# Splitting both last-phase projection weights once, in token block 2, and keeping the halves in DRAM

## The chip, the cores and the metric

The kernel runs on one core of a Trainium2 chip, in one launch. The metric is device time in microseconds (us), the median of several runs. The engines are named as in the profile: PE (matrix engine), PEld (its weight loads), DVE (vector engine), ACT (scalar engine), POOL (GpSimd) and SP (the sync engine, which issues all DMAs of this kernel; its rows read SPq).

## The reference

A decoder block over 2048 tokens of 1024 channels, all in float32. Both branches read one normalised and modulated input through one input projection. Cut to what matters here:

```python
h = _rmsnorm(x, norm_g[l]) * (1.0 + scale[:, None, :]) + shift[:, None, :]
p = jnp.einsum('bsd,de->bse', h, w_in[l])
c_val, c_gate, c_og, ts, r_og, g_conv, g_rwkv = jnp.split(p, SPLITS, axis=-1)
y_conv = _conv_branch(c_val, c_gate, c_og, ..., w_conv_out[l])   # ends in u @ w_conv_out
y_rwkv = _rwkv7_branch(ts, r_og, ..., w_rwkv_out[l])             # ends in o @ w_rwkv_out
m = jax.nn.sigmoid(g_conv) * y_conv + jax.nn.sigmoid(g_rwkv) * y_rwkv
out = jnp.einsum('bsd,de->bse', m, w_out[l])
x = x + gate[:, None, :] * out
return _rmsnorm(x, final_g)
```

The convolution branch ends in a layer norm over channels and a gate; the RWKV branch is a recurrence over tokens with a state of 64 x 64 per head, a group norm and a gate.

## The kernel before

Tokens are worked in four blocks of 512 (b = 0 to 3). A float32 product is made of three products of halves: every weight and every activation is split into a high half (a cast to fp32r) and a low half (the difference), and `mm3` adds hi x hi, hi x lo and lo x hi. A weight of 128 output channels is a tile of 128 x 1024 values (0.5 MB).

The first phase runs over the blocks. Each makes its input h (`hprep`, from x that `xnorm` normalised and stored a block earlier), then goes through four groups (g) of four heads: `pair` projects k, r and v and prepares the chunks of the recurrence; `group` inverts small triangular matrices on POOL (through DRAM: dA, La, dT) and runs the recurrence; `fill` does convolution (`conv`) and gate (`gates`) projections beside it. Input weights are split in block 0 and kept in DRAM (`KEPT`); later blocks load both halves (kh_in, kl_in, lines 168 and 169). The buffers called hx (seven of 128 x 512) serve the normalisation of x. In block 1 they also serve `ogate`, which multiplies the output weight by its gate, splits it and stores the halves (kh_o, kl_o): in each group two weights, each in two pieces of 128 x 512, here called halves of a weight. Block 3 has no next block to normalise, and does the first parts of the last phase's block 0 there.

The last phase starts while the last recurrence ends. For each block: `osplit` (RWKV output, gate, split), `lnorm` (layer norm of the convolution, gate, split), `rproj` (product with w_rwkv_out, eight weights, "ro"), `cproj` (with w_conv_out, eight weights, "co"), and the output product ("pout", eight pieces of weight, 48 products each) with the final norm (`addx`, `finish`). `rproj` and `cproj` call `load_w`, which for "ro" and "co" loads the weight (line 172), casts the high half on ACT (line 175) and subtracts on DVE (line 177), in every block anew. High, low and unsplit tiles share six buffers (tag "w", `WB = 6`).

Inside each engine instructions run in a fixed order. It is made when the kernel is built, by a scheduler that estimates times; `tc.high_priority` moves an instruction ahead. DMAs are issued by SP in its order, and an issue that waits for its source or its buffer holds all those behind it.

Of the kernel before, what the change touches and what calls it, by code (L numbers as in the profile page):

```python
# [9 lines left out]
F32 = mybir.dt.float32  # L10
F32R = mybir.dt.float32r
I32 = mybir.dt.int32
AF = mybir.ActivationFunctionType
ALU = mybir.AluOpType
# [4 lines left out]
P = 128  # L19
D = 1024  # L20
KT = D // P
# [26 lines left out]
def lplan(t):  # L48
    n = {"c": 0, "g": 0}
    r = []  # L50
    for part in t.split():
        l = []
        for w in part:
            if w != "-":
                l.append(("1234" if w == "g" else w, n[w]))
                n[w] += 1
        r.append(l)
    return r
# [24 lines left out]
def hybrid_block(ctx: ExitStack, tc: tile.TileContext, x, vecs, convk, w2a2, final_g, ada, w_in, w_co, w_ro, w_o, crow, out,  # L83
                 seq=2048, groups=(0, 1, 2, 3), phase2=True, dbg=None):
    nc = tc.nc
# [6 lines left out]
    dp = ctx.enter_context(tc.tile_pool(name="dp", bufs=1, space=DRAM))  # L92
# [43 lines left out]
    wsrc = {"in": w_in, "co": w_co, "ro": w_ro, "o": {(cb, kh): w_o[cb, kh] for cb in range(4) for kh in range(2)}}  # L136
# [6 lines left out]
    kept = {}  # L143
# [3 lines left out]
    def ogate(n, half):  # L147

        back = kept.setdefault(("o", n), [dp.tile([P, KT, P], F32R, name=f"k{p_}_o{n[0]}_{n[1]}", tag=f"k{p_}_o{n[0]}_{n[1]}")
                                          for p_ in "hl"])  # L150
        hs = slice(half * 4, half * 4 + 4)
        st, gr, hi, lo = hx("w_st"), hx("w_gr"), hx("w_hi"), hx("w_lo")
        nc.sync.dma_start(st.rearrange("p (k n) -> p k n", k=4), wsrc["o"][n][:, hs, :])
        nc.sync.dma_start(gr[:, :256], grow_d[n[0] * 256:n[0] * 256 + 256].unsqueeze(0).broadcast_to([P, 256]))
        s4 = st.rearrange("p (k n) -> p k n", n=256)
        nc.gpsimd.tensor_tensor(out=s4, in0=s4, in1=gr[:, :256].unsqueeze(1).broadcast_to([P, 2, 256]), op=ALU.mult)
        nc.scalar.copy(hi.bitcast(F32R), st)
        nc.gpsimd.tensor_tensor(out=lo.bitcast(F32R), in0=st, in1=hi, op=ALU.subtract)
        for d_, s_ in zip(back, (hi, lo)):
            nc.sync.dma_start(d_[:, hs, :].bitcast(F32), s_.rearrange("p (k n) -> p k n", k=4))  # L160
# [151 lines left out]
    for g in range(4):  # L312
        s_ = c1.tile([P, 2, P], F32, name=f"S{g}")
# [3 lines left out]
    def hx(name):  # L317
        return xp.tile([P, TB], F32, name=name, tag="hx")

    def xnorm(b, tts=range(NTT)):  # L320
        for tt in tts:
            t0 = b * TB + tt * P
            ss = e2.tile([P, 8], F32, name="ss")
            xh = []
            for half in range(2):
                xt = hx("xt")
                nc.sync.dma_start(xt, x[t0:t0 + P, half * TB:half * TB + TB])
                nc.scalar.activation(hx("xsq"), xt, AF.Square, accum_out=ss[:, half:half + 1])
                xh.append(xt)
            vs, rs = ss[:, 2:3], ss[:, 3:4]  # L330
            nc.vector.tensor_tensor(out=vs, in0=ss[:, 0:1], in1=ss[:, 1:2], op=ALU.add)
            nc.vector.tensor_scalar(out=vs, in0=vs, scalar1=1.0 / D, scalar2=RMS_EPS, op0=ALU.mult, op1=ALU.add)
            rsqrt(rs, vs, e2, nc.vector, ss[:, 4:5])
            for kh in range(2):
                nc.vector.tensor_scalar(out=xh[kh], in0=xh[kh], scalar1=rs, scalar2=None, op0=ALU.mult)
                pt = pl.tile([P, 4, P], F32, name="late", tag="late")
                for i in range(4):
                    nc.tensor.transpose(pt[:, i, :], xh[kh][:, i * P:(i + 1) * P], ident)
                xo = hx("xTs").rearrange("p (a b) -> p a b", a=4)
                for i in range(4):  # L340
                    k = kh * 4 + i
                    nc.scalar.activation(xo[:, i, :], pt[:, i, :], AF.Identity, scale=g_col[:, k:k + 1],
                                         bias=shift_col[:, k:k + 1])
                nc.sync.dma_start(xT_dram[b][:, kh * 4:kh * 4 + 4, tt * P:(tt + 1) * P], xo)
# [10 lines left out]
    def hprep(b):  # L355
        h = ([], [])
        for k in range(KT):
            hf = hx("hf")
            nc.sync.dma_start(hf, xT_dram[b][:, k, :])
            hsplit(h, k, hf)  # L360
        return h
# [454 lines left out]
    def z_first(js):  # L816
        for j in js:
            z, bt = hx("z"), hx("zb")
            nc.sync.dma_start(z, o_dram[0][j])
            nc.sync.dma_start(bt, bv_dram[0][j])  # L820
            nc.gpsimd.tensor_tensor(out=z, in0=z, in1=bt, op=ALU.add)
            rt = hx("zr")
            nc.sync.dma_start(rt, ro_dram[0][j])
            nc.gpsimd.tensor_tensor(out=z, in0=z, in1=rt, op=ALU.mult)
            nc.sync.dma_start(z_dram[j], z)

    def lora_split(h):

        lf, ll, lx = hx("lora"), hx("lora_lo"), hx("lora_x")
        shifted(h, T_LORA, lf)  # L830
        nc.scalar.activation(lf[0:64], lf[0:64], AF.Tanh)
        lw = e1.tile([P, TB], F32R, name="lw", tag="lw")
        la = e1.tile([P, TB], F32R, name="la", tag="la")
        lo_, hi_ = slice(0, 64), slice(64, 128)
        for dst, sl, os_ in ((lw, lo_, hi_), (la, hi_, lo_)):
            nc.scalar.copy(dst[sl], lf[sl])
            nc.vector.tensor_tensor(out=ll[sl], in0=lf[sl], in1=dst[sl].bitcast(F32), op=ALU.subtract)
            nc.sync.dma_start(lx[os_], ll[sl])
            nc.scalar.copy(dst[os_], lx[os_])
        return lw, la  # L840
# [3 lines left out]
    def ada_steps():  # L844
        for k, _ in enumerate(ada_cols(srow, l3, "As", ASB, [((k, 8 + k), (mod[:, k:k + 1], mod[:, 8 + k:9 + k]))
                                                             for k in range(KT)])):
            ks, gs = slice(k, k + 1), slice(8 + k, 9 + k)
            nc.vector.tensor_tensor(out=shift_col[:, ks], in0=mod[:, ks], in1=ab[:, ks], op=ALU.add)
            nc.vector.tensor_tensor(out=g_col[:, ks], in0=mod[:, gs], in1=ab[:, gs], op=ALU.add)
            nc.vector.scalar_tensor_tensor(out=g_col[:, ks], in0=g_col[:, ks], scalar=1.0, in1=vc("norm_g", k),  # L850
                                           op0=ALU.add, op1=ALU.mult)
            yield

    for b in range(NB):
        h = hprep(b) if b else hprep0(x0, ada_steps())
        lora = lora_split(h)
        for g in groups:
            if b + 1 < NB:
                xnorm(b + 1, XN[g])
            else:  # L860
                z_first(ZN[g])
                if g < 3:
                    lnorm_first(g)
            if b + 1 < NB:
                todo = [(w, 2 * g + m) for w, m in (FIRST if b == 0 and g == 0 else NEXT)]
            else:
                todo = [wj for i in range(g, 4 if g < 3 else 5) if i == g or g == 3 for wj in lplan(LP)[i]]

            if b == 1:
                for _ in range(2):  # L870
                    n_ = later.pop(0)
                    for half in range(2):
                        ogate(n_, half)

            def fill(step, n=None):
                for _ in range(n or (FILL0[step] if b == 0 and g == 0 else 0)):
                    w, j = todo.pop(0)
                    if w == "c":
                        conv(b, h, j)
                    else:  # L880
                        gates(b, h, j, w)

            wcount[0] = WSH
            group(b, g, h, lora, fill)
            if b == 0 and g == GG:
                for _ in ada_cols(srow, l3, "As", ASB, [((16 + k, 17 + k), (hgate_col[:, k:k + 1], hgate_col[:, k + 1:k + 2]))
                                                        for k in range(0, KT, 2)]):
                    pass
                nc.vector.tensor_tensor(out=hgate_col, in0=hgate_col, in1=ab[:, 16:24], op=ALU.add)
                nc.vector.tensor_scalar(out=hgate_col, in0=hgate_col, scalar1=0.5, scalar2=None, op0=ALU.mult)  # L890
                nc.sync.dma_start(grow_d.rearrange("(n p) -> p n", p=P), hgate_col)
            wcount[0] = WDVE
            if todo:
                fill(0, len(todo))
# [75 lines left out]
    hl = ctx.enter_context(tc.tile_pool(name="hl", bufs=1, reuse_waits="tile"))  # L970
# [54 lines left out]
    for b in range(NB):  # L1025
# [7 lines left out]
        for tt in range(NTT):  # L1033
            xh = []
            for half in range(2):
                n = 2 * tt + half
# [97 lines left out]
```

## Time and profile before

| | us |
|---|---|
| time, median of 3 runs | 3144.74 (3140.74 to 3146.39) |
| span of the profiled execution, first to last instruction | 3131.2 |
| token block 1 of the first phase (672 to 1272) | 600 |
| token block 2 of the first phase (1272 to 1866) | 594 |
| last phase, from about 2494 to the end | 637 |

The profile gives the profiled execution's span; its time around the span isn't shown apart, and the median lies 13.5 us above the span. A row of the stretches gives its length, the busy time of each engine with the count of its instructions, the granted clock of PE (1.00 is full speed), the busy share of the DMA engines and what they moved. A row of waits reads: who waited, for whom, us in total, times, longest. A row in order of time reads: start, length, engine and line, operation, output and inputs, count, and the idle time before with what ended it.

### The profile page before, as it was taken

The page shows a single profiled execution, that of the slowest core. Times are in us where ns is not written, and L with a number is a line of the kernel's source. Part 1 is how long each engine was busy: PE and PEld are TensorE (multiplying, and loading weights), DVE is VectorE, ACT ScalarE, POOL GpSimd, SP SyncE. Part 2 cuts the span into 40 slices and gives each one's busy share as a digit, 9 for nine tenths or more (in the row PEclk, how much of TensorE's full clock was granted, in tenths as well). Part 3 has the DMA queues.
Part 4 walks back from the last instruction along what each step waited for, and adds up shares of the span by engine and source line. Part 5 has one row for each costly group of instructions (what it writes and reads, how often), then busy time and mean ns, then how long its engine had stood idle before and what let it go on. Part 6 is the DMA issues. An engine that isn't in the chain of part 4 may idle for free.

```text
span 3131.2 us, 64840 instructions
## 1 busy us (share of the span) xinstructions
PE 2990.4 (96%) x25672; PEld 2808.5 (90%) x25672; DVE 2169.9 (69%) x4326; ACT 1045.9 (33%) x1887; POOL 1125.1 (36%) x1692
## 2 busy tenths in 40 slices
PE   6799998999999999999999999999999999699998
PEld 5789998999999999999999999999999988487888
DVE  6686877676767665867667586758598455977643
ACT  4424333333323242423142324132332223343421
POOL 3354545424342424141313235326256014643100
PEclk9899999999999999999999999999999999899999
DMA  8665758563747476545546557636457657756554
GB/s 300 215 240 191 259 199 275 195 235 126 256 141 244 150 244 216 190 156 182 178 164 194 186 193 243 198 130 214 137 166 262 215 174 264 261 198 232 189 185 158
DMA packets 343328, 638.42 MB, mean 204 GB/s; under 512 B 133424, under 2 KB 152176, under 8 KB 343024
## 3 DMA queue, kind: packets, MB, share of 16 engines
q1 hardware_dynamic: 343024, 634.27, 60.4%
q8 instruction: 202, 3.31, 0.4%
q14 instruction: 102, 0.84, 0.1%
HBM read 462.10 MB, written 170.92 MB: 202 GB/s over the span
## 4 chain that ended last, share of the span: by engine, by line
PE 71%; DVE 10%; DMA 9%; POOL 4%; issue 2%; SPq 2%; ACT 2%; DVEq 0%; POOLq 0%; ACTq 0%
PE ps_main L192 50%; PE aux L522 3%; PE xo L679 2%; PE xo L650 2%; PE xo L670 2%; DMA w_st<-w_in_t 2%; PE xo L665 2%; PE xo L685 2%; PE pout L1055 1%; POOL TT L593 1%; PE pout L1056 1%; PE pout L1054 1%; POOL itmp L591 1%; DVE acc L756 1%; DMA w_gr<-grow_d 1%
## 5 line engine op out<-in xcount | busy, mean ns | idle before, releaser
L192 PE MATMUL ps_main<-h_hi,w_hi 128*128 128x256 f32 x4608 | 954.9, 285 | 23.1 <-ACT w_hi L175 19.7
L192 PE MATMUL ps_main<-h_hi,w_lo 128*128 128x256 f32 x4608 | 959.1, 285 | 8.1 <-POOL w_lo L177 6.6
L192 PE MATMUL ps_main<-h_lo,w_hi 128*128 128x256 f32 x4608 | 959.0, 285 | 0.0
L192 PEld LDWEIGHTS ps_main<-h_hi,w_hi 128*128 128x128 f32 x4608 | 718.8, 190 | 33.6 <-ACT w_hi L175 20.8
L192 PEld LDWEIGHTS ps_main<-h_hi,w_lo 128*128 128x128 f32 x4608 | 717.2, 189 | 17.9 <-POOL w_lo L177 8.2
L192 PEld LDWEIGHTS ps_main<-h_lo,w_hi 128*128 128x128 f32 x4608 | 717.7, 189 | 6.8 <-issue 0.5
L756 DVE SCALAR_TENSOR_TENSOR acc<-u,ck,acc 128x512 f32<-128x512 f32 x928 | 697.9, 752 | 20.4
L175 ACT CAST w_hi<-w_st 128x1024 fp32r<-128x1024 f32 x135 | 141.5, 1048 | 327.7 <-DMA w_st<-w_in_t 120.8
L591 POOL TENSOR_TENSOR itmp<-La,TT 128x126 f32<-128x126 f32 (+22 forms) x496 | 179.8, 363 | 137.4 <-DMA La<-dA 102.1
L690 DVE SCALAR_TENSOR_TENSOR S<-xo,pe,Se 64x64 f32<-64x64 f32 x512 | 144.8, 283 | 108.4 <-PE xo L685 99.1
L593 POOL TENSOR_TENSOR TT<-TT,itmp 128x126 f32<-128x126 f32 (+22 forms) x496 | 191.9, 387 | 36.0
L177 DVE TENSOR_TENSOR w_lo<-w_st,w_hi 128x1024 fp32r<-128x1024 f32 x88 | 117.8, 1339 | 110.0 <-PE ps_main L192 53.7
L660 ACT ACTIVATE Se<-S,pe 128x128 f32<-128x128 f32 x256 | 89.1, 394 | 232.7 <-DVE S L690 232.3
L177 POOL TENSOR_TENSOR w_lo<-w_st,w_hi 128x1024 fp32r<-128x1024 f32 x47 | 112.5, 2394 | 136.2 <-ACT w_hi L175 83.5
L545 POOL TENSOR_TENSOR vv<-rk,vv 128x512 f32<-128x512 f32 x32 | 43.2, 1350 | 324.4 <-ACT rk L544 324.4
L681 DVE TENSOR_TENSOR uv<-xo,rn 64x256 f32<-64x256 f32 x128 | 53.9, 421 | 129.7 <-PE xo L679 128.7
L522 PE MATMUL aux<-KR,BKz 128*128 128x128 f32 x1024 | 139.9, 282 | 2.8 <-DVE As L524 2.1
L522 PEld LDWEIGHTS aux<-KR,BKz 128*128 128x128 f32 x1024 | 126.2, 194 | 5.7 <-DVE As L524 2.4
L524 DVE TENSOR_TENSOR As<-aux,maskA 128x512 f32<-128x512 f32 x128 | 86.8, 687 | 52.8 <-PE aux L522 51.9
L673 DVE COPY X<-xo 64x256 f32<-64x256 f32 x128 | 53.6, 419 | 89.5 <-PE xo L670 88.6
L652 ACT COPY uv<-xo 64x256 f32<-64x256 f32 x128 | 46.8, 365 | 175.7 <-PE xo L650 175.2
L665 PE MATMUL xo<-S,KR 128*128 128x128 f32 x512 | 96.4, 280 | 6.9 <-DVE S L690 6.7
(294 smaller groups left out, 5464.1 us busy)
## 6 DMA issues: line engine op xcount, KB each, us to landing
w_hi<-kh_in SPq DMA_DIRECT2D x219, 512.0 KB, 3.8
w_lo<-kl_in SPq DMA_DIRECT2D x219, 512.0 KB, 4.9
w_st<-w_in_t SPq DMA_DIRECT2D x73, 512.0 KB, 4.4
kh_in<-w_hi SPq DMA_DIRECT2D x71, 512.0 KB, 2.9
kl_in<-w_lo SPq DMA_DIRECT2D x71, 512.0 KB, 4.3
w_st<-w_ro_t SPq DMA_DIRECT2D x32, 512.0 KB, 3.9
w_st<-w_co_t SPq DMA_DIRECT2D x32, 512.0 KB, 3.5
w_hi<-kh_o SPq DMA_DIRECT2D x32, 512.0 KB, 3.6
```

Source lines behind the costliest of these rows:

```text
L175: nc.scalar.copy(hi, st)
L177: lo_eng.tensor_tensor(out=lo, in0=st, in1=hi.bitcast(F32), op=ALU.subtract)
L192: nc.tensor.matmul(ps[:, qs], ww[:, k, :], aa[k][:, qs], start=(k == 0 and t == 0 and q == 0), stop=(k == KT - 1 and t == 2 and q == ms - ...
L522: nc.tensor.matmul(pA[:, c // 2, es], BKz[:, hh, cc, es], KR[:, cc, es], start=(c == 0), stop=(c == 3), skip_group_check=True)
L524: nc.vector.tensor_tensor(out=Asb[:, hh, c4 * 4:c4 * 4 + 4, :].rearrange("p (a e) n -> p a (e n)", e=2), in0=pA, in1=flat(maskA).unsqueeze ...
L591: nc.gpsimd.tensor_tensor(out=tmp[:, :ni, :nt], in0=La[:, j:j + 1, j + 1:].broadcast_to([P, ni, nt]), in1=TT[:, :ni, j:j + 1].broadcast_to ...
L593: nc.gpsimd.tensor_tensor(out=TT[:, :ni, j + 1:], in0=TT[:, :ni, j + 1:], in1=tmp[:, :ni, :nt], op=ALU.add)
L650: nc.tensor.matmul(xo[vr, q, hs], As[q][:, hh, c, rc], uv[:, c, q, hs], start=False, stop=(q == 1 and hh == 1), skip_group_check=True)
L660: nc.scalar.mul(Se[:, q, :], Sg[:, q, :], R[q]["pe"][:, c:c + 1])
L665: nc.tensor.matmul(xo[:, q, :], R[q]["KR"][:, cc, es], Sg[:, q, :], start=(q == 0), stop=False, skip_group_check=True)
L690: nc.vector.scalar_tensor_tensor(out=Sg[hs, q, hs], in0=xo[hs, 2 + q, hs], scalar=R[q]["pe"][hs, c:c + 1], in1=Se[hs, q, hs], op0=ALU.mult ...
L756: nc.vector.scalar_tensor_tensor(out=acc if i + 1 < HALO else yj, in0=u[:, i:i + TB], scalar=ck[:, j, i:i + 1], in1=acc, op0=ALU.mult, op1 ...
```

## The change

`ro` and `co` weights are treated as the output weights are. In token block 2, each group takes four weights (first the eight of "ro", then the eight of "co"), and `keep` loads each in two halves of 128 x 512 into hx buffers, casts on ACT, subtracts on POOL and stores both results in DRAM. `load_w` then finds them in `kept` in all four blocks of the last phase and loads two tiles of 0.5 MB; the load, the cast and the subtraction of lines 172 to 177 remain for input weights in block 0 only.

```diff
+    pending = [(name, n) for name in ("ro", "co") for n in range(KT)]
+
+    def keep(name, n, half):
+        back = kept.setdefault((name, n), [dp.tile([P, KT, P], F32R, name=f"k{p_}_{name}{n}", tag=f"k{p_}_{name}{n}")
+                                           for p_ in "hl"])
+        hs = slice(half * 4, half * 4 + 4)
+        st, hi, lo = hx("w_st"), hx("w_hi"), hx("w_lo")
+        nc.sync.dma_start(st.rearrange("p (k n) -> p k n", k=4), wsrc[name][n][:, hs, :])
+        nc.scalar.copy(hi.bitcast(F32R), st)
+        nc.gpsimd.tensor_tensor(out=lo.bitcast(F32R), in0=st, in1=hi, op=ALU.subtract)
+        for d_, s_ in zip(back, (hi, lo)):
+            nc.sync.dma_start(d_[:, hs, :].bitcast(F32), s_.rearrange("p (k n) -> p k n", k=4))
...
+            if b == 2:
+                for _ in range(4):
+                    n_ = pending.pop(0)
+                    for half in range(2):
+                        keep(*n_, half)
```

Lines from the new function on are 13 higher than before (18 higher in the last phase): line 168 becomes 181, 577 becomes 590, 907 becomes 925, 1021 becomes 1039. What the scheduler makes of it is shown at three places.

SP in the last group of token block 2, around the input weight kh_in71 (w_hi and w_lo are the weight's two tiles, dA carries the triangular matrices to DRAM, La brings them back, bv is a result). Before:

```order
L168 DMA w_hi_22935<-kh_in55_7809 128x1024
L169 DMA w_lo_22936<-kl_in55_7810 128x1024
L577 DMA dA_22338<-As_21752 32x4x32 x8
L546 DMA bv_d2_7_122<-vv_22249 128x512
L582 DMA La_22356<-dA_22338 64x1024 x2
L168 DMA w_hi_22992<-kh_in71_7872 128x1024
L169 DMA w_lo_22993<-kl_in71_7873 128x1024
```

and now, just ahead of the same weight:

```order
L173 DMA kh_co4_21990<-w_hi_22003 128x512
L169 DMA w_st_22012<-w_co_t 128x512
L590 DMA dA_22658<-As_22072 32x4x32
L173 DMA kl_co4_21991<-w_lo_22004 128x512
L590 DMA dA_22658<-As_22072 32x4x32 x2
L559 DMA bv_d2_7_122<-vv_22569 128x512
L173 DMA kh_co5_22010<-w_hi_22013 128x512
L169 DMA w_st_22022<-w_co_t 128x512
L590 DMA dA_22658<-As_22072 32x4x32
L173 DMA kl_co5_22011<-w_lo_22014 128x512
L181 DMA w_hi_23312<-kh_in71_7872 128x1024
L182 DMA w_lo_23313<-kl_in71_7873 128x1024
```

All 16 halves of "co" stand in this one run, between the weight loads of the third and fourth group, five of them between kh_in55 and kh_in71; the loads of block 3's input (hf), which stood ahead of the run's place, now follow it. The 16 halves of "ro" stand in two runs of eight, at the start of the first and the second group.

SP where the last phase's block 1 begins its layer norm (o_d: last results of the recurrence; kh_o: output weight; y: the convolution's result; bt, rt, ot: inputs of `osplit`; ct: the gate). Before:

```order
L724 DMA o_d3_6_97<-oc_29826 128x512
L168 DMA w_hi_32273<-kh_o2_0_12431 128x1024
L169 DMA w_lo_32274<-kl_o2_0_12432 128x1024
L724 DMA o_d3_7_98<-oc_29834 128x512
L975 DMA fg_31753<-final_g 128x1024
L985 DMA y0_31852<-y_d1_0_171 128x512
```

Now:

```order
L737 DMA o_d3_6_97<-oc_30146 128x512
L181 DMA w_hi_32495<-kh_o1_1_10532 128x1024
L182 DMA w_lo_32496<-kl_o1_1_10533 128x1024
L737 DMA o_d3_7_98<-oc_30154 128x512
L993 DMA fg_32041<-final_g 128x1024
L1003 DMA y0_32140<-y_d1_0_171 128x512
```

The last transposes of the recurrence, whose results o_d stores, stand behind 25 and 53 of the first block's output products on PE (before: 78 and 108), and the layer norm's loads follow the fourth pair of output weights rather than the fifth.

DVE in the middle of `rproj` of block 1 (w_lo: a split's subtraction; mr: a projection's result taken from PSUM; y: the layer norm; u_lo: the low half of its result; o_lo: `osplit` of block 2). Before:

```order
L1008 TENSOR_SCALAR dg_31927<-ident_308,rv_31914 128x128 x4
L177 TENSOR_TENSOR w_lo_32730<-w_st_32731,w_hi_32729 128x1024
L957 SCALAR_TENSOR_TENSOR mr3_32586<-rth_32693,ps_main_32701 128x512
L907 TENSOR_TENSOR o_lo6_33177<-ot_33251,o_hi6_33178 128x512
L202 SCALAR_TENSOR_TENSOR y0_31852<-th_31941,y0_31852 128x512
L1021 TENSOR_TENSOR y0_31852<-y0_31852,ct_31938 128x512
L957 SCALAR_TENSOR_TENSOR mr4_32587<-rth_32727,ps_main_32735 128x512
L202 SCALAR_TENSOR_TENSOR y1_31854<-th_31951,y1_31854 128x512
L907 TENSOR_TENSOR u_lo_31937<-y0_31852,u_hi_31936 128x512
```

Now:

```order
L925 TENSOR_TENSOR o_lo4_33437<-ot_33487,o_hi4_33438 128x512
L975 SCALAR_TENSOR_TENSOR mr2_32873<-rth_32943,ps_main_32949 128x512
L215 SCALAR_TENSOR_TENSOR y0_32140<-th_32229,y0_32140 128x512
L1039 TENSOR_TENSOR y0_32140<-y0_32140,ct_32226 128x512
L215 SCALAR_TENSOR_TENSOR y1_32142<-th_32239,y1_32142 128x512
L925 TENSOR_TENSOR u_lo_32225<-y0_32140,u_hi_32224 128x512
L1039 TENSOR_TENSOR y1_32142<-y1_32142,ct_32236 128x512
L215 SCALAR_TENSOR_TENSOR y2_32145<-th_32249,y2_32145 128x512
L975 SCALAR_TENSOR_TENSOR mr3_32874<-rth_32975,ps_main_32981 128x512
```

No subtraction of a split is left there, and the layer norm's tail begins behind mr2, where it began behind mr3.

## The prediction, made before the changed kernel had run

> **What bounds the kernel now.** I read the page first (the span, the engines), then the busy time by stretch, then who waited for whom, and last the matrix engine's and the DMA queue's own rows in order of time.
>
> ```profile
> span 3131.2 us, 64840 instructions
> PE 2990.4 (96%) x25672; PEld 2808.5 (90%) x25672; DVE 2169.9 (69%) x4326; ACT 1045.9 (33%) x1887; POOL 1125.1 (36%) x1692
> ```
>
> The matrix engine (PE) is busy for 96% of the span, so a change pays only where PE stands still or runs at the half clock. The last phase begins at about 2494 us. Its stretches: the tail of the recurrence with the first block's projections; the first block's output product; the second block's projections (the RWKV and the convolution weights, 2656 to 2791); its output product with the third block's projections; the rest.
>
> ```profile
> core 0: us, PE busy (x) PEld busy (x) DVE busy (x) ACT busy (x) POOL busy (x), PEclk, DMA share, GB/s
> 2494.00:2601.00 107.00, 107.00 (x553) 85.91 (x553) 60.26 (x97) 31.97 (x52) 16.85 (x11) 0.99 0.57 192
> 2601.00:2656.00 55.00, 50.68 (x398) 49.38 (x397) 25.85 (x58) 20.62 (x50) 29.81 (x23) 0.94 0.81 287
> 2656.00:2791.00 135.00, 104.53 (x404) 79.17 (x404) 112.31 (x161) 46.63 (x66) 75.60 (x47) 0.90 0.65 223
> 2791.00:2940.00 149.00, 142.18 (x784) 121.07 (x783) 116.74 (x191) 67.56 (x114) 55.18 (x36) 0.98 0.65 219
> 2940.00:3131.00 191.00, 180.62 (x1151) 162.84 (x1150) 80.58 (x203) 42.79 (x97) 0.00 (x0) 0.98 0.51 178
> ```
>
> PE stands still for 30.5 us in the third row, 6.8 in the fourth, 4.3 in the second, and not at all in the first. The fifth row's 10.4 us are the closing store chain, which the change does not touch. In the third row the granted clock is 0.90 too. What ended those waits, in 2601:2791 and then in 2791:2940:
>
> ```profile
> PE ps_main L192 <- DVE w_lo L177: 21.3, 7, 5.5
> PE ps_main L192 <- ACT w_hi L175: 6.9, 3, 4.6
> PE pout L1054 <- DMA w_hi<-kh_o: 3.8, 1, 3.8
> ...
> PE ps_main L192 <- DVE rs L130: 5.5, 2, 3.9
> ```
>
> 28.2 of the 30.5 us are waits for a split: PE wants a weight's low half, whose subtraction on the vector engine (DVE) stands behind other work. DVE is the bound there, 112 of 135 us busy. This is what the change takes away. The time of the split by stretch (DVE's column):
>
> ```profile
> 2656.00:2791.00 135.00, 23.88 (x16) 0.00 (x0) 0.90 0.65 223
> 2940.00:3131.00 191.00, 19.59 (x16) 0.00 (x0) 0.98 0.51 178
> ```
>
> **The change, part by part.** The sum is made against the profiled span; 3144.74 is the median, so 13.5 us lie around the span and I shift the span's change onto the median.
>
> *Removed from the last phase:* 64 casts and 64 subtractions. In three of the five stretches they end no wait of PE's, and are worth nothing. In 2656:2791 they are 23.9 us of DVE time, and DVE's remaining 88.4 us is less than the 92 us that PE needs there: 384 products at 0.233 us, and a few small ones. The spacing comes from PE's starts, 6 steps from the first to the second row; an output product takes 0.118 us, 8 steps from the third to the fourth:
>
> ```profile
> 2599.65 0.40 PE L192 MATMUL ps_main<-o_hi,w_lo 128*128 128x512 f32 x1
> ...
> 2601.05 0.39 PE L192 MATMUL ps_main<-o_hi,w_lo 128*128 128x512 f32 x1
> 2601.28 0.28 PE L1054 MATMUL pout<-w_hi,o_hi 128*128 128x256 f32 x1
> ...
> 2602.22 0.28 PE L1056 MATMUL pout<-w_hi,o_lo 128*128 128x256 f32 x1
> ```
>
> So DVE stops being the bound, if its order lets the normalisation follow at once.
>
> *What comes late next: the DMA.* Each of these weights now moves 1 MB (two halves) rather than 0.5 MB. The stretch from the last store of the recurrence to the last convolution weight of the second block:
>
> ```profile
> 2615.94 0.32 SPq L724 DMA_DIRECT2D o_d<-oc  x1
> 2616.31 0.42 SPq L975 DMA_DIRECT2D fg<-final_g  x1
> ...
> 2616.00:2761.00 145.00, 110.21 (x545) 89.48 (x544) 113.63 (x165) 56.00 (x96) 101.89 (x67) 0.88 0.74 258
> ...
> 2620.00:2640.00 20.00, 15.68 (x112) 15.18 (x111) 3.69 (x6) 3.28 (x10) 14.33 (x12) 0.84 1.03 390
> ...
> 0.00:50.00 50.00, 23.01 (x156) 20.45 (x156) 39.48 (x112) 22.58 (x39) 12.50 (x22) 1.00 0.82 323
> ...
> 2600.00:2650.00 50.00, 45.68 (x354) 44.43 (x353) 21.48 (x43) 18.53 (x45) 24.00 (x18) 0.93 0.82 296
> ```
>
> That is 145 us at 258 GB/s, 37.4 MB. The change adds 16 x 0.524 = 8.4 MB and, by the order on the queue, one more pair of output weights (1.05 MB): 46.9 MB. By the order of PE's instructions the last transposes of the recurrence stand behind 53 output products rather than 108, 55 x 0.118 = 6.5 us earlier, so the stretch begins near 2609.4. Then 46.9 MB takes 120 us at 390 GB/s (the best 20 us, the queue never empty), 145 us at 323 (the best 50 us), 158 us at 296 (50 us of this very place). One weight's products (5.6 us) follow the last landing: the second block's projections end at 2740 (bounded there by PE: 39 + 92 us of products from 2609.4), 2760 or 2773, where they now end at 2791. I take 323 GB/s, since the place has neither an always full queue nor today's waits for the split: a gain of 31 us, between 18 and 51.
>
> The Trainium skill, DMA: Bandwidth & Descriptors, section "Where 436 GB/s comes from", has the HBM side bind transfers to and from SBUF at about 358 GB/s per core. By it the 46.9 MB would take 131 us and the gain would be an estimated 45 us. The row with 390 GB/s for 20 us does not bear it out as a ceiling for this lone core.
>
> *The third block's projections* (2791:2940): the two waits of 5.5 us stand behind subtractions and the output's small operations on DVE. There, 32.6 MB become 41 MB in 149 us, 275 GB/s, below the rates above. The gain is between 0 and 8 us (the waits and the half clock behind them); I take 5.
>
> *New waits on PE:* PE takes its instructions in order, and in the new order the second block's mean, variance and broadcast products stand earlier (the mean behind 214 output products, before 266). Where the normalisation is not ready, PE stands. Also the fifth pair of output weights now stands behind the 15 loads that the sixth stood behind: the 4.3 us wait stays. I take 5 us, between 0 and 10.
>
> *Added in block 2:* 32 halves, each with a load, a cast (0.62 us), a POOL subtraction (1.31 us) and two stores. PE has no room there (593 of 594 us), so every delay counts. The nearest work is block 1's, which does nearly the same to 16 halves of the output weights. Stretch and parts:
>
> ```profile
> 672.00:1272.00 600.00, 592.75 (x5566) 570.42 (x5563) 409.11 (x880) 193.48 (x371) 210.95 (x387) 1.00 0.61 200
> 1272.00:1866.00 594.00, 592.99 (x5634) 572.32 (x5634) 415.10 (x889) 185.75 (x358) 173.12 (x356) 1.00 0.54 177
> ...
> L158 POOL TENSOR_TENSOR w_lo<-w_st,w_hi 128x512 fp32r<-128x512 f32 x16 | 21.0, 1310 | 7.3 <-ACT w_hi L157 7.3
> ...
> L157 ACT CAST w_hi<-w_st 128x512 fp32r<-128x512 f32 x16 | 9.9, 620 | 47.5 <-POOL w_st L156 44.3 <-DMA w_hi<-kh_in 3.3
> ...
> w_st<-w_o_t SPq DMA_DIRECT2D x16, 256.0 KB, 4.8
> ```
>
> Block 1 takes 600 us and block 2 takes 594, with 7.25 and 1.0 us of idle PE: 16 halves cost about 6.2 us. POOL's added work is equal (32 operations in either), the transfers are less than doubled, so 32 halves cost between 6.2 and 12.5 us, or 0 if block 1's waits have another cause. I take 8, nearer to the equal POOL work. The Trainium skill, GPSIMD Engine Reference, section "8. Key points", says that GpSimd shares its SBUF interfaces with VectorE and contends with its two-input instructions. The split's rows agree: 23.88 / 16 = 1.49 us with POOL half busy, 1.22 us with POOL idle. By that rule the added POOL work would stretch DVE in block 2 by an estimated 12 us (42 us of POOL, DVE 70% busy, 40% slower while both run), which its 179 idle us hide unless it falls on the recurrence's chain.
>
> *Sum:* -31 - 5 + 5 + 8 = -23 us: the span 3108, the median about 3122.
>
> **The rivals.** *A, the DMA takes back what the split gave.* If the stretch keeps today's 258 GB/s, because loads stand in one queue behind buffers that DVE frees, 46.9 MB takes 182 us and ends at 2797: no gain there. With +5 for the third block, no other new wait, and block 2's 8 us, the time is 3144.7 - 5 + 8 = about 3148: no change. Against it: with the queue never empty the same place moved 390 GB/s for 20 us; the rate is low where SP waits for buffers that the waiting PE and DVE hold.
>
> *B, slower: the queue in block 2.* SP issues in order, and the store of a half's high part waits for its cast, which waits for its load. So each half holds SP for a period p. In block 1:
>
> ```profile
> 825.14 0.32 SPq L160 DMA_DIRECT2D kh_o<-w_hi  x1
> 825.52 0.86 SPq L153 DMA_DIRECT2D w_st<-w_o_t  x1
> ...
> 833.58 0.32 SPq L160 DMA_DIRECT2D kh_o<-w_hi  x1
> ...
> 841.58 0.32 SPq L160 DMA_DIRECT2D kh_o<-w_hi  x1
> ...
> SPq L160 <- ACT w_hi L157: 51.7, 15, 6.4
> ...
> 1420.83 0.69 SPq L168 DMA_DIRECT2D w_hi<-kh_in  x1
> ...
> 1471.09 0.80 SPq L577 DMA_DIRECT2D dA<-As  x2
> ...
> 1738.89 0.32 SPq L168 DMA_DIRECT2D w_hi<-kh_in  x1
> ...
> hf<-xT SPq DMA_DIRECT2D x24, 256.0 KB, 6.0
> ...
> 1866.81 1.33 ACT L350 CAST h_hi<-hf 128x512 fp32r<-128x512 f32 x2
> ```
>
> There p was 8.2 us, with the gate's load and product in it. Without these I get 0.4 + 4.8 + 0.6 = 5.8 us. The convolution weights' 16 halves stand in one run behind the load of 1738.9, from about 1745 us, and block 3's inputs (hf) now stand behind them; block 3's first cast was at 1866.8. At 5.8 us the run ends at 1838, in time. At 8.2 it ends at 1876, and hf lands some 6 us later: PE stands for 15 us. The first two groups (8 halves each, 66 us where SP had 50, 1421 to 1471) come 16 us late, of which two weights loaded ahead (2 x 5.6 us) cover 11, and lose 5 each: 25 us in place of 8. With 31 us won later the change is then nearly a wash, and above p of about 8.4 it is a loss; at 9 us (run to 1889, hf 28 us late, 11 in each of the two groups) the price is 50 us and the time about 3164. For it: casts in ACT's queue wait for others, up to 6.4 us. Against it: the gate's product, which ended 44.3 of the cast's 47.5 us of waiting, is gone.
>
> *C, more than forecast:* the DMA keeps its 390 GB/s and PE is the bound; -51 - 8 + 8 gives about 3094.
>
> **How the numbers follow.** Forecast (gain of 7 to 42) 0.66, A 0.15, B 0.12, C 0.07. About 0.2% (6 us) is what a measurement of this kernel can tell from no change. Faster: 0.66 + 0.07 + a little of A = 0.74; the same 0.14; slower 0.12. The low end is the forecast's best sum without C's whole gain, 3144.7 - 51 + 8 = 3102; the high end is A with block 2 at 12.5 us, about 3150.
>
> **What would show it.** Right: no wait of PE for L175 or L177's successors after 2494 us, DVE some 85 us and ACT some 66 us less busy there; the second block's projections about 100 us long; a DMA share near 0.85 in them. In block 2, SP's waits for the new cast at 3 us or less each, PE idle below 10 us. Wrong: PE waits for kh_ro or kh_co landings that sum to over 20 us (A); block 3's first cast later than block 2's last product, or waits for kh_in in block 2 beyond 15 us (B); a stall of over 10 us at the second block's mean or variance.

## The result, and the profile after

The change makes the kernel faster: 3109.22 us (median of 4 runs, 3106.85 to 3111.5) against 3142.74 us of the kernel before (4 runs on the same chip, 3137.01 to 3146.39). The ratio is 0.9895, with a 95% interval of 0.9881 to 0.9909: 33.5 us, where 23 were forecast and the range ran from 3102 to 3150.

First the page's head, the span and the busy time of each engine:

```profile
span 3106.3 us, 65042 instructions
PE 2983.5 (96%) x25672; PEld 2802.6 (90%) x25672; DVE 2088.0 (67%) x4262; ACT 997.6 (32%) x1855; POOL 1152.3 (37%) x1724
```

DVE has 82 us less to do, ACT 48, POOL 27 more. PE's share is 96% as before: the span shrank by what PE no longer waits, not by work taken from it.

Then the busy time by stretch, cut at the first output product of a block (the prediction cut in other places, so the first row is the kernel before, by the new cut, and the next is the kernel after in the same stretch; then the third block's stretch and the rest, after):

```profile
2601.00:2791.00 190.00, 155.21 (x801) 128.55 (x801) 138.16 (x218) 67.25 (x116) 105.41 (x69) 0.91 0.69 241
```

```profile
2609.00:2771.00 162.00, 147.72 (x800) 123.30 (x800) 105.87 (x179) 50.96 (x100) 97.65 (x69) 0.97 0.92 334
2771.00:2915.00 144.00, 140.80 (x782) 119.74 (x782) 97.54 (x189) 51.39 (x98) 53.62 (x36) 0.99 0.81 289
2915.00:3106.00 191.00, 180.53 (x1154) 162.73 (x1152) 62.31 (x187) 26.11 (x81) 0.00 (x0) 0.98 0.62 219
```

From the first output product of the last phase to that of its second block, 190 us became 162. PE has the same 800 instructions in it, but is busy with them for 147.7 us rather than 155.2: its granted clock rose from 0.91 to 0.97. (The clock's records in these two traces hold only full and half speed: 34.1 us at half speed in the first stretch, 10.2 in the second.) Beside it DVE went from 138 to 106 us and the DMA engines from 241 to 334 GB/s, a share of 0.69 to 0.92: they are now busy for most of the stretch. What still holds PE there, in that stretch of the kernel after:

```profile
PE ps_main L205 <- DVE mr L975: 5.0, 3, 2.8
PE ps_main L205 <- ACT u_hi L924: 4.0, 2, 2.6
PE pout L1072 <- DMA w_hi<-kh_o: 2.8, 1, 2.8
PE pout L1073 <- DMA w_lo<-kl_o: 0.8, 1, 0.8
PE ps_main L205 <- DMA w_lo<-kl_ro: 0.8, 1, 0.8
```

The 28.2 us of waits for a split are gone, and 14.3 us of idle PE are left where there were 34.8. Of these, 5.0 us are waits until DVE has taken a projection's result out of PSUM (`mr`), 4.0 us are waits for a half of the layer norm's result (`u_hi`), and 4.4 us are landings of weights. So the 28 us of the stretch are 20.5 us of idle time and 7.5 us of PE time at the lower clock. The lower clock went with the idle time in this pair of kernels; no run varied one without the other.

To place the whole difference I cut the span at the first cast of h in a block and at the first output product of each block of the last phase (2601.28 before, 2609.05 after):

| us | block 0 | block 1 | blocks 2 and 3, to the first output product | last phase from there | PE idle in that |
|---|---|---|---|---|---|
| before | 672.8 | 600.0 | 1328.4 | 529.9 | 41.6 |
| after | 680.2 | 600.6 | 1328.2 | 497.3 | 17.5 |

The last phase has 32.7 us less, and the median 33.5. Blocks 1 to 3 together are unmoved, although block 2 got the whole splitting. Block 0, whose instructions are the same in the same order, is 7.4 us longer in the profiled run after; in all the other kernels that follow (but the one with fewer weight tiles) it takes 677.7 to 682.2, so it was the profiled run before that was quick there. This also corrects a reading of the prediction: after, the profiled run took 3108.03 us with a span of 3106.3, so only 1.7 us lie around the span. The 13.5 us between the span and the median before were mostly the difference between two runs. One run of the third-tile kernel below took 3549.47 us at a granted clock of 0.77; it is left out of that kernel's range.

### The profile page after: what moved, and what is told of

The parts are those of the page before. It is cut to its first block, busy times and chain, and to the rows that moved or that the text cites. A ratio compares the mean times of both kernels' runs of the same rounds, so it can differ in the third digit from the quotient of the medians.

```text
span 3106.3 us, 65042 instructions
## 1 busy us (share of the span) xinstructions
PE 2983.5 (96%) x25672; PEld 2802.6 (90%) x25672; DVE 2088.0 (67%) x4262; ACT 997.6 (32%) x1855; POOL 1152.3 (37%) x1724
## 4 chain that ended last, share of the span: by engine, by line
PE 69%; DMA 11%; DVE 9%; POOL 5%; ACT 2%; SPq 2%; issue 2%; DVEq 0%; ACTq 0%; POOLq 0%
PE ps_main L205 48%; PE aux L535 3%; DMA w_st<-w_in_t 3%; PE xo L692 2%; PE xo L663 2%; PE xo L683 2%; PE xo L678 2%; POOL TT L606 2%; PE xo L698 1%; POOL itmp L604 1%; PE pout L1073 1%; PE pout L1072 1%; PE pout L1074 1%; DMA w_st<-w_ro_t 1%; DMA w_gr<-grow_d 1%
## 5 line engine op out<-in xcount | busy, mean ns | idle before, releaser
L205 PE MATMUL ps_main<-h_hi,w_hi 128*128 128x256 f32 x4608 | 957.9, 286 | 28.2 <-ACT w_hi L188 23.3
L188 ACT CAST w_hi<-w_st 128x1024 fp32r<-128x1024 f32 x71 | 74.4, 1048 | 168.6 <-DMA w_st<-w_in_t 131.9
L431 ACT ACTIVATE t<-ps_main,mu 128x512 f32<-128x512 f32 x96 | 65.8, 686 | 90.9 <-PE ps_main L205 80.6
```

The source lines that it names most:

```text
L188: nc.scalar.copy(hi, st)
L205: nc.tensor.matmul(ps[:, qs], ww[:, k, :], aa[k][:, qs], start=(k == 0 and t == 0 and q == 0), stop=(k == KT - 1 and t == 2 and q == ms - ...
L431: nc.scalar.activation(t1, ps, AF.Identity, scale=mu1[:, mi:mi + 1])
```

## The experiments

Three theories were put against each other: that the waits for the split made the time (the prediction's); that it was the third tile, which the unsplit weight took from the rotating buffers; and, for what was paid, that block 2's work costs 6 to 12 us. The last phase is read as in the table above, from PE's rows in order of time. Each ratio is against runs of the kernel before that were made beside it; their medians lie between 3140.73 and 3141.51 us.

| kernel | us (range) | ratio to before, 95% | last phase | PE idle in it |
|---|---|---|---|---|
| block 2's work only | 3151.3 (3135.98 to 3154.03) | 1.0024 (1.0010 to 1.0039) | 540.0 | 46.4 |
| last phase only | 3114.1 (3107.29 to 3122.47) | 0.9914 (0.9897 to 0.9931) | 505.4 | 24.3 |
| RWKV weights only | 3107.12 (3102.71 to 3111.74) | 0.9892 (0.9876 to 0.9908) | 500.0 | 19.3 |
| convolution weights only | 3123.4 (3119.58 to 3133.1) | 0.9946 (0.9929 to 0.9963) | 518.2 | 32.2 |
| third load | 3137.49 (3133.95 to 3149.71) | 0.9993 (0.9982 to 1.0005) | 528.7 | 38.7 |
| third tile | 3130.42 (3124.28 to 3142.32) | 0.9971 (0.9959 to 0.9983) | 519.2 | 30.9 |
| low halves on POOL | 3167.0 (3163.51 to 3177.57) | 1.0095 (1.0080 to 1.0110) | 560.1 | 68.0 |
| kept late | 3118.14 (3114.92 to 3122.44) | 0.9935 (0.9922 to 0.9947) | 498.4 | 20.1 |
| two ahead | 3341.3 (3338.3 to 3345.58) | 1.0636 (1.062 to 1.0653) | 538.3 | 45.0 |
| RWKV kept in block 2, convolution kept late | 3113.81 (3102.74 to 3115.17) | 0.9906 (0.9889 to 0.9922) | 501.5 | 21.2 |

**Block 2's work only.** The halves are made and stored, but the last phase does not find them and splits anew:

```diff
+    spare = {}
     def keep(name, n, half):
-        back = kept.setdefault((name, n), ...)
+        back = spare.setdefault((name, n), ...)
```

> Block 2 splits and stores both weights as in the changed kernel, but the last phase does not use the halves and splits anew, as before; the instructions up to the last phase stand in the changed kernel's order. My price of block 2's work (8 us, 6.2 to 12.5): slower than the kernel before by 0.2 to 0.4%. Rival, from the changed kernel's trace (first cast of block 2 to the first output product took 1329 us in both kernels): 0, no difference.

It is slower by 0.24% (3 to 12 us), which is the forecast's number, but not by the forecast's cause. In its profile blocks 2 and 3 take 1328.9 us (1328.4 before), and the loss stands in the last phase (540.0 against 529.9), where the instructions are those of before and only their order was planned anew. The waits in the second block's stretch of the last phase are the old ones again:

```profile
PE ps_main L206 <- DVE w_lo L191: 18.4, 5, 5.4
PE ps_main L206 <- ACT w_hi L189: 10.3, 3, 6.4
```

28.7 us, as the 28.2 of before. So this kernel does not price block 2's work cleanly. Seven profiles do: blocks 2 and 3 took 1328.2, 1328.9, 1324.4 and 1328.4 us in the kernels with the whole added work (after, this one, third load, third tile) and 1328.4, 1327.7 and 1327.0 in those without (before, last phase only, low halves on POOL). The means are 1327.5 and 1327.7 us: the price is 0 within about 2 us. Why the planned order of this kernel's last phase came out some 10 us worse stays open. Every kernel below has an order of its own in the last phase too, so a difference of some 10 us between two of them can be the order's.

**Last phase only.** The kernel before, whose last phase loads halves that are in DRAM already (those of sixteen input weights), so that block 2 does nothing more:

```diff
-        back = kept.get((name, n))
+        back = kept.get(("in", n + (8 if name == "co" else 0)) if name in ("ro", "co") else (name, n))
```

> The last phase loads two finished tiles per weight, but they are halves of the input weights that block 0 kept (the right weights are left out, nothing is split in block 2); up to the last phase the order is that of the kernel before. If the whole gain is the last phase's and block 2 is free: the changed kernel's time, 33 us below the kernel before. If block 2 costs 8 us: some 41 us below. If the changed kernel gained something ahead of the last phase too: clearly less than 33 us.

It gains 27 us (22 to 32) with the last phase's side alone: the gain comes from there. That it is not faster than the full change also fits block 2's work costing next to nothing. Its last phase is 8 us longer than the change's, and one wait for DVE to take a result out of PSUM is long here (second block's stretch); whether that is the order's doing was not tested:

```profile
2604.00:2774.00 170.00, 148.84 (x796) 125.47 (x796) 106.05 (x179) 50.05 (x99) 91.89 (x68) 0.92 0.89 319
...
PE ps_main L192 <- DVE mr L957: 11.9, 1, 11.9
```

**RWKV weights only, and convolution weights only.** Half of the change each, two weights per group of block 2:

```diff
-    pending = [(name, n) for name in ("ro", "co") for n in range(KT)]
+    pending = [(name, n) for name in ("ro",) for n in range(KT)]      # or ("co",)
...
-                for _ in range(4):
+                for _ in range(2):
```

> Only the eight RWKV output weights are split in block 2 and kept; the convolution's are split in the last phase as before. By PE's waits before (7 of 8 waits for a split of over 1 us in the RWKV projections of the second block, 25 of 30 us), the theory that the split waits in PE's path gives two thirds or more of the gain, 22 us or more. Rival, that the gain is DVE time freed, whichever weight it is: half, 16 us.

> Only the eight convolution weights are kept; the RWKV weights are split in the last phase as before. Waits in PE's path: a third of the gain or less, below 11 us. DVE time freed, whichever weight: half, 16 us; though in the second block DVE has these subtractions later than the layer norm, so they could be worth less than half here too.

The RWKV weights alone bring the whole gain (34 us), the convolution weights alone half (17 us): the parts don't add. The first result fits the theory of PE's path (22 us or more) and not its rival (16); the second fits the rival (16) and not the theory (below 11). So neither theory holds alone. Second block's stretch with the RWKV weights alone:

```profile
2610.00:2779.00 169.00, 150.65 (x802) 126.83 (x801) 118.99 (x202) 58.51 (x107) 101.97 (x69) 0.94 0.84 296
...
PE pout L1073 <- DMA w_lo<-kl_o: 5.1, 1, 5.1
PE ps_main L205 <- DVE mr L975: 4.6, 3, 2.5
PE pmean L1008 <- POOL ys L1006: 3.6, 1, 3.6
```

No wait for a split is left here either, though the eight convolution weights are still split. With the eight RWKV weights arriving split, DVE (119 of 169 us) is ahead with the others. With both sets kept this stretch is 7 us shorter (162) and the next one 4 us longer. The convolution weights still take three tiles each here, and the gain is whole even so.

With the convolution weights alone, the same stretch takes 177 us and keeps these waits for a split:

```profile
PE ps_main L205 <- DVE w_lo L190: 8.9, 3, 5.0
PE ps_main L205 <- ACT w_hi L188: 5.1, 2, 3.9
```

All 14.0 us are for RWKV weights, which are split here as before; in the kernel before, some 24 of the 28.2 us were theirs. So taking other subtractions off DVE, busy for 119 us here where it was 138, also shortens the waits for a split that stays.

**Third load.** After, where each of these weights also loads 0.5 MB into a third tile that nothing reads: the tile that a weight took before and 0.5 MB more than after, with no split.

```diff
         if back is not None:
+            if name in ("ro", "co"):
+                ex = whl.tile([P, KT, P], F32, name="w_ex", tag="w", bufs=WB)
+                nc.sync.dma_start(ex, back[0].bitcast(F32))
```

> The changed kernel, with a third load of 0.5 MB for each RWKV and convolution weight in the last phase, into a third tile of the six buffers that nothing reads. If the DMA is now the bound in the second block's stretch (changed kernel: share 0.92, 334 GB/s from 2609 to 2771 us), 16 loads there cost 16 x 1.3 = 21 us or more, and the next stretch (share 0.81, 289 GB/s) some more: slower than the changed kernel by 20 to 35 us. If DVE's chain is the bound: under 10 us. The third tile alone is told apart by the next run.

The gain is gone: 28 us are lost against the change, within the 20 to 35 expected. The second block's stretch and its waits:

```profile
2605.00:2785.00 180.00, 153.29 (x801) 127.69 (x800) 110.55 (x196) 55.84 (x109) 106.09 (x75) 0.91 0.96 350
...
PE ps_main L208 <- DMA w_lo<-kl_ro: 11.0, 4, 3.9
PE ps_main L208 <- DMA w_hi<-kh_ro: 5.1, 2, 2.7
PE ps_main L208 <- DVE rs L125: 5.1, 1, 5.1
```

PE waits for landings (16.1 us) in place of splits, with the DMA engines at 350 GB/s and 0.96 of their time. The DMA takes the gain back here, as the forecast's rival A has it, though not by rival A's mechanism: that kept the rate at 258 GB/s, while here the rate rose and the bytes with it. Tile and bytes came together, so the next kernel parts them.

**Third tile.** The same third tile, with 64 bytes per partition loaded into it rather than 4 KB:

```diff
+                nc.sync.dma_start(ex[:, 0, 0:16], back[0][:, 0, 0:16].bitcast(F32))
```

> The changed kernel, with the third tile of the run before but only 64 bytes of each partition loaded into it: two weights ahead in the six buffers as before the change, not three. If the three-deep prefetch matters, slower than the changed kernel by 5 to 15 us; if two weights ahead are enough: within 4 us of it.

```profile
2608.00:2779.00 171.00, 152.09 (x804) 128.32 (x803) 101.63 (x180) 50.53 (x100) 96.86 (x68) 0.94 0.91 319
...
PE ps_main L208 <- DMA w_lo<-kl_ro: 8.4, 4, 3.3
PE pout L1075 <- DMA w_hi<-kh_o: 5.2, 1, 5.2
```

With next to no added bytes 21 of the 33 us are lost (24 by the ratios), more than the 5 to 15 expected; the bytes of the third load cost only 7 more. With three tiles a weight, the six buffers hold two weights; with two tiles, three. So the loads reach less far ahead, which can explain the loss, and PE's 8.4 us of waits for low halves that landed late fit it. But the dummy tile does one thing more. In the last phase SP also waits for the landing of the dummy (`w_ex`), which the kernels without it don't have:

```profile
SPq L182 <- DMA w_ex<-kh_co: 29.5, 20, 4.1
SPq L182 <- DMA w_ex<-kh_ro: 9.2, 8, 2.0
```

These are 38.7 us in which the queue stood still (2608 to 3127 us), and the order was planned anew as well. So the kernel shows that a third tile with a small load can lose most of the gain; how much of the 21 us is the reach, how much the dummy's landings and how much the order stays open. The RWKV-only kernel, where half of the weights still take three tiles and nothing is lost, speaks against a fixed price of the tile.

**Low halves on POOL.** The other remedy for a busy DVE, in the kernel before:

```diff
-W2 = 4
+W2 = 0
```

> The kernel before, with the last phase's 64 subtractions on POOL rather than DVE (2.4 us each rather than 1.3). If the split cost time by DVE's load, much of the gain comes without any work in block 2: 10 to 20 us below the kernel before. If what counts is that the split stands in a queue in PE's path at all, POOL (56% busy in the second block's stretch, and in the path of the layer norm) makes it no better or worse: 0 or slower by up to 20 us.

It is 0.95% slower, 30 us, beyond the 20 that the second theory allowed. The second block's stretch:

```profile
PE ps_main L192 <- DVE mr L957: 11.8, 1, 11.8
PE ps_main L192 <- DVE rs_t L129: 11.8, 1, 11.8
PE ps_main L192 <- POOL w_lo L177: 8.9, 2, 7.5
PE ps_main L192 <- ACT w_hi L175: 5.5, 2, 3.2
```

PE still waits for the split, and now also for DVE, although 16 subtractions left DVE in this stretch, 24 us before. DVE's busy time fell by only 14 us (to 123.7), while POOL's rose from 105 to 136. The trace shows a reason. Here are two runs of one small step of the final norm (`rs_t`, one value per partition) and POOL's split:

```profile
2656.77 2.30 DVE L128 TENSOR_TENSOR rs_t<-rs 128x1 f32<-128x1 f32 x1
2656.68 2.38 POOL L177 TENSOR_TENSOR w_lo<-w_st,w_hi 128x1024 fp32r<-128x1024 f32 x1
2669.38 0.15 DVE L128 TENSOR_TENSOR rs_t<-rs 128x1 f32<-128x1 f32 x1
```

The step takes 0.15 us with POOL idle and 2.30 us beside the split, and it ends as the split ends (2659.07 and 2659.06). Eight such steps of the norm in this stretch took 0.98 to 2.30 us, each ending within 0.02 us of the end of a POOL instruction. So the split on POOL held DVE there, and the wait for it was moved, not removed.

**Kept late.** Nothing in block 2; the halves are stored when the last phase's first block has split them:

```diff
-KEPT = ("in",)
+KEPT = ("in", "ro", "co")
```

> The kernel before, but its first block of the last phase stores both halves after its split and the three later blocks load them; block 2 does nothing new. The waits of the second and third block go as in the changed kernel (32 us), and no time of block 2 is used; against it, 16 weights' stores, 16.8 MB, go into 2494 to 2601 us, which moves 192 GB/s now and would move 349. If the DMA bears that: the changed kernel's time. If not: slower than the changed kernel by 5 to 20 us.

Its last phase (498.4 us) is as short as the change's, its time 9 us longer, within the 5 to 20 of the second case. Seven of those 9 us stand ahead of the first output product (blocks 2 and 3 take 1335.0 us), where the last recurrence overlaps the first block's projections with their splits and stores.

**Two ahead.** After, with four weight tiles rather than six (`WB = 4`): two weights ahead, without a dummy tile.

> The kernel after with four weight tiles in the rotating pool rather than six: two weights ahead instead of three, no third tile, no added bytes. The split is gone from the last phase as in the kernel after. It is read by the last phase (first output product to end: 530.0 us before, 497.2 after, 519.1 with the third tile held and hardly filled), since fewer tiles also change the blocks ahead. Theory (depth): the reach of the loads ahead is worth some 20 us, so the last phase takes 511 to 527 us, its added waits are for landings of the weights. Rival (the split alone): what the third tile cost was the order that it forced on the queue, not the depth; the last phase stays at 495 to 505 us. The whole time is 3120 to 3145 by the theory if blocks 0 to 2 are unmoved, and 3105 to 3115 by the rival.

The blocks ahead suffer too (block 0 takes 771.9 us), so only the last phase is read: 538.3 us, 41 more than after, beyond the 14 to 30 that the theory of depth gave, and far from the rival's 495 to 505. There is no split at all in it, and it is no shorter than before the change. So four buffers cost time without any dummy, but not the amount that the theory gave. Waits in the second block's stretch:

```profile
PE ps_main L205 <- DVE xt L1093: 8.6, 1, 8.6
PE pout L1072 <- DMA w_hi<-kh_o: 8.5, 2, 7.4
PE ps_main L205 <- DVE xt L1080: 4.9, 1, 4.9
PE ps_main L205 <- DMA w_hi<-kh_ro: 3.6, 3, 1.7
PE ps_main L205 <- DMA w_lo<-kl_co: 3.3, 2, 2.2
```

The output weights, which bring no dummy tile with them in the run before, lose a third of their buffers here as well, which goes with the 8.5 us for kh_o; the waits for `xt`, with the output's own work on DVE, were not taken apart.

**RWKV kept in block 2, convolution kept late.** The RWKV-only kernel with `KEPT = ("in", "co")`, as a try at a version that beats the change:

> The RWKV weights are split in block 2 as in the kernel with these alone (3107.1 us), and the convolution weights' halves are stored in the last phase when its first block has split them, for the later blocks to load. Theory: after these RWKV weights the rest of the split ends next to no wait (the kernel with RWKV weights alone had 18.4 us of idle PE in the second block's stretch against 14.3 with both), and the tail of the split is worth at most 4 us while its stores add 8.4 MB to a phase whose DMA share is near 0.9: the same within 5 us, 3102 to 3112. Rival: the convolution weights' low halves still hold PE at the third and fourth block, and the third tile still costs a weight of reach there: faster by 5 to 12 us, 3095 to 3102. The other rival: the added stores hold the queue in the last phase's first block, slower by 5 to 12 us, as late keeping of both weights was against early keeping (3118 against 3109).

3113.81 us, 2 us outside the range of the theory, with an interval that overlaps those of the RWKV-only kernel and of the change: no better. None of the kernels beats the change by more than its interval; the RWKV weights alone equal it with half the added work.

## Why the prediction was right, point by point

**The bound, and what goes.** Right: PE's waits for the split in 2601 to 2791 were the place, and no wait for a split is left after 2494 us. Of the 33 us, 28 fell there. DVE has 80 us less to do in the last phase and ACT 59 (85 and 66 were forecast; the cut is at 2494 in both, although the kernel after reaches the same point of its work some 8 us later).

**The second block's stretch, forecast -31 and +5 for new waits.** Measured -28, against the -26 of the two terms. That the sum came so close is in part luck. The stretch it was made for, from the last store of the recurrence to the last convolution weight, was read too short: in the kernel before, three of the eight convolution weights were issued after its end at 2761, the last at 2773.5, and up to about 2779, where that one lands, 40.0 MB moved and not 37.4. With the 9.5 MB that the prediction adds, these are 49.5 MB; at the 323 GB/s taken they need 153 us, and the gain would have been 23 us, not 31. The rate was taken too low as well. The kernel after moves 50 MB in the same 145 us from its last store of the recurrence:

```profile
2618.00:2763.00 145.00, 130.72 (x686) 107.77 (x685) 98.87 (x169) 47.99 (x95) 97.06 (x68) 0.96 0.95 345
```

The two errors cancel. The projections alone take 109 us (2662 to 2771) where about 100 were forecast and 135 stood. New waits were there, some 9 us, near the top of their range, but not at the place named: the mean, variance and broadcast products cost 0.3 us, and the waits stand where the results leave PSUM and where the layer norm's halves are wanted. The choice between 258 and 390 GB/s was decided by the right argument, that the DMA could do more than today's rate: a queue with more bytes ran faster. But the mechanism was only half named: the prediction put the gain down to DVE's path, and saw the freed buffers only as a reason for a better rate. The third-tile kernel, with no split in PE's path and the buffers held, gets some 9 us (5 to 13 by its interval). How much of the rest is the buffers' is open, for the reasons given there; a kernel that still splits, but from a buffer outside the six, was not run.

**The third block, forecast -5.** Measured -4.4 over two stretches together, from the second block's first output product to the fourth's (283.9 to 279.4 us). The later of the two, shown here, became shorter only because one weight's products, 24 of them at 0.233 us, had slipped into it before:

```profile
2934.00:3075.00 141.00, 140.87 (x793) 122.26 (x794) 65.21 (x135) 35.24 (x66) 0.00 (x0) 1.00 0.57 193
```

```profile
2915.00:3050.00 135.00, 135.00 (x769) 117.50 (x768) 42.69 (x112) 17.33 (x48) 0.00 (x0) 1.00 0.69 247
```

The first row is before, the second after: 793 instructions of PE against 769.

**Block 2's work, forecast +8, the step that failed.** It costs 0 within about 2 us. The price was taken from block 1's being 6.2 us longer than block 2, on the reading that its 16 halves made the difference; twice as many halves then cost nothing, so that reading does not hold, as the prediction had allowed. What makes block 1 longer was not tested. The queue's part of it was right. The stores of the convolution weights' high halves in block 2, and SP's waits from 1270 to 1880 us:

```profile
L173 SPq DMA_DIRECT2D kh_co<-w_hi x16: 319/320/537, 1760.1 to 1843.2; - x16
...
SPq L181 <- PE ps_main L205: 189.4, 52, 10.1
SPq L173 <- ACT w_hi L170: 59.7, 28, 6.0
...
SPq L173 <- POOL w_lo L171: 7.2, 15, 0.7
```

Sixteen halves from 1760.1 to 1843.2 us are 5.5 us each; 5.8 was forecast, and 8.2 would have made it a wash (rival B). SP's waits for the cast are 2.1 us on average, with one of 6.0 where 3 was the bound named. They seem not to have delayed PE because they stand in time that SP spent waiting for PE anyway: the wait for PE to free a weight's buffers was 284.4 us before (1262 to 1872), and is 189.4 now.

```profile
SPq L168 <- PE ps_main L192: 284.4, 60, 10.1
```

95 us less of waiting for free buffers paid for the 67 us of waiting for casts and subtractions. Block 3's inputs were issued from 1843.6 us, and its first cast began at 1880.8, 6 us later than before when block 0's 7.4 us and block 1's 0.6 are taken off, with no idle PE from 1872 to 1892 us.

The Trainium skill, GPSIMD Engine Reference, section "8. Key points", would have had POOL's 42 us of new work stretch DVE in block 2 by an estimated 12 us. The trace agrees at most by half. Block 2 before had 415.10 us in 889 of DVE's instructions, 467 ns each; after it is this row, 474 ns each, some 6.5 us in all:

```profile
1280.00:1874.00 594.00, 590.37 (x5583) 567.85 (x5582) 412.29 (x869) 201.09 (x387) 213.62 (x388) 1.00 0.66 215
```

**The rivals.** A (today's rate stays) is refuted by 334 GB/s. Putting a third tile and its load back takes the gain away, but at 350 GB/s, so not by A's mechanism. C (390 GB/s, PE the bound) did not come: 345 GB/s over the stretch in question, and PE still idle for 14.3 us.

**The sum.** -28 - 4.4 + 0 for block 2 gives -32.4, the measured 33.5 less a run's scatter; the forecast of -23 was short mainly by the 8 us. (The high end of the range, A with 12.5 us for block 2, adds up to 3152 rather than 3150.)

## What to carry to other kernels

When PE waits for a conversion that runs between a load and a product, count the buffers that the conversion holds beside its time: putting a third tile back without the split lost 21 of the 33 us here. But look at the queue before calling that the tile's price: a dummy that must land holds the queue itself, and each edit brings a new order, which alone was worth 10 us in one kernel. Work beside a full engine can be free if the in-order queue that carries it has waits of its own to give: here 67 us of new waits stood against 95 us of old ones that went. Compare the two, and see that the next phase's inputs still come in time. Moving work from DVE to POOL can hold DVE instead of freeing it: look at DVE's small steps while POOL is busy. And do first the part that the waits name; half of this change had all of its gain.

## What the runs showed of the hardware

A single core held 334 GB/s over 162 us and 350 GB/s over 180 us of loads with some stores, the DMA engines busy for 0.92 and 0.96 of the time, where the same place had 241 at 0.69 in the kernel before: the low rate was the program's. The Trainium skill, DMA: Bandwidth & Descriptors, section "Where 436 GB/s comes from", has about 358 GB/s as what the HBM side allows a core. These runs do not bear it out as a ceiling for a core that works alone: shorter stretches went beyond it, in the kernel after (first row) and with the third load (second row).

```profile
2681.00:2731.00 50.00, 39.93 (x163) 29.78 (x162) 36.63 (x36) 17.83 (x27) 33.12 (x23) 0.98 1.03 389
```

```profile
2686.00:2786.00 100.00, 84.11 (x332) 64.98 (x331) 51.82 (x76) 25.80 (x41) 50.99 (x36) 0.90 1.00 372
```

A DVE step of one value per partition and two inputs, 0.15 us with POOL idle, took up to 2.30 us beside POOL's subtraction and ended with it (the kernel with the low halves on POOL).

Block 0, the same instructions in the same order, took 672.8 us in the profiled run before and 680.2 in that after. One profiled span can be 10 us off its median in a kernel whose runs agree within 0.3%, so a gain of 30 us is read from the stretch and not from two spans.
